# Raw weights and keys' copies issued by ScalarE, six output weight blocks split in the last pair, and shared buffers for parts of the softmax units, in a one-core attention layer

## The chip, the core and the metric

The kernel runs on one core of a Trainium2 chip. The core has five engines, each with its own queue of instructions that it works through strictly in order: TensorE (PE, matmuls and weight loads), VectorE (DVE), ScalarE (ACT), GpSimd (POOL) and SyncE (SP, which here only issues DMAs). [...] An instruction that has to wait holds up everything behind it in its queue. The metric is the device time of one execution in microseconds (us), as the median of several runs.

## The reference

One transformer-like layer on a sequence of 1024 rows with 1024 features, all float32. Two attention groups of eight heads each read the same normalised input: softmax attention with a forget gate, and stick-breaking attention. Their outputs pass a SiLU gate and one output projection, and a residual with a final layer norm ends it.

```python
u = layer_norm(x) * (1 + scale) + shift            # shift, scale, gate from silu(c) @ w_ada + b_ada
fq, fk, fv, fg, ff, sq, sk, sv, sg = split(u @ w_in)
# softmax group, per head:   s = q k^T / 8 + (f_q - f_k), causal;  p = softmax(s);  o = p v
# stick-breaking, per head:  z = q k^T / 8;  w = exp(log_sigmoid(z) + sum of later log_sigmoid(-z));  o = w v
y = concat(o_fox * silu(fg), o_sb * silu(sg)) @ w_out
out = layer_norm(2 ** 0.25 * x + gate * y) * ln_g + ln_b
```

## The kernel before, in words

Precision: most float32 products are made of rounded parts. A matrix is split into a high part (rounded) and a low part (the rest), and three matmuls (high by high, low by high, high by low) stand for one. `fetch_w` (L134) does this for weights: a DMA brings a raw block of 128x512 into one of two `wraw` buffers, POOL rounds it into `whi` (L141) and subtracts to get `wlo` (L142); the five-deep ring `whi`/`wlo` feeds PE. For output weights POOL first multiplies the raw block by the gate (L139).

Heads are worked in eight pairs; pairs 0 to 3 are stick-breaking, pairs 4 to 7 softmax. A pair has 16 units: one unit is one head and one block of 128 queries, `i` from 0 to 7, and its row of scores is (i+1)*128 wide. Pairs 0 to 3 go through the blocks upwards, pairs 4 to 6 downwards, widest first.

One softmax unit (`att_scores`, L492, and `halves`, L474) goes like this. PE makes the scores `S` (L504, L505) in one of two PSUM buffers. DVE reads them with the forget term `fb` into `a` and finds the row bound `nm` (L511). ACT takes the exponential (L517). ACT and DVE make two 16-bit halves of the result in a buffer `f` (L483, L484). SP issues a transposing DMA from `f` to `pt` (L488). Four units later PE multiplies `pt` by the values (`pv`, L582). Both `a` and `f` come from a ring of six buffers named `att`, which also holds `fb`; a buffer is free again when its last reader is done, for `f` the transposing DMA. A stick-breaking unit uses `kp` and `be` from the same ring, with a scan on DVE and a product on POOL (L538).

Between the matmuls of the units PE is given "filling" work: the projections of later pairs (`gen_m`, lines L288 to L290, `m`, which produce queries, keys and gates; `gen_v`, L359 to L361, `v`, values). A table FILL says how many steps of filling each pair gets, and a weight per unit says how they are spread over its 16 units. `v_finish` scales the values; it ends in a small matmul `vsum` (L397) that waits for DVE. `forget_rows` makes the cumulated forget gates (`fcum`, L431), for which POOL prepares a triangle of ones first. The order of PE's instructions is written out by hand; on DVE, ACT, POOL and SP the framework's scheduler orders them, by its own estimate of when each is ready.

Keys (`evac_k`) are copied by ACT out of PSUM, and a small DMA copies each half to the other 64 partitions (L270, issued by SP). Values and other big buffers share a ring `v` of three 8 KB buffers.

Output weights: from the end of pair 3 through pair 6 `gen_split_out` (L927) fetches all eight blocks of `w_out` in two halves each, splits them on POOL and stores both parts to a DRAM scratch `wo_dr` (L933, L934). In the last pair, PE's filling is the last gate projection (`gen_last_g`), step `kt` by step. Each step frees the buffers `u{kt}` and `v{kt}` (the normalised input), and `load_wo(kt)` brings block `kt` back from `wo_dr` into them (L924, L925). Then the output projection (`o_step`, L986 to L988) of row tile 6 begins, `gen_out_first`, block by block, and the other seven row tiles follow. `load_y` brings the stored gated outputs back and splits them on POOL, through the same `wraw` and `whi`/`wlo` buffers.

## Time and profile before

| | |
|---|---|
| median of 3 runs | 699.71 us (699.4 to 701.07) |
| the profiled execution | 706.99 us, of which the span from first to last instruction is 705.3 us |
| mean granted TensorE clock in it | 0.956 of full speed |
| DVE busy | 497.7 us (71%) |
| ACT busy | 397.1 us (56%) |
| POOL busy | 414.3 us (59%) |
| first scores of pairs 0, 4, 5, 6, 7 | at 89.6, 340.5, 423.2, 492.6 and 565.0 us |

How to read it: the profile page lists, for the whole span, the busy time of each engine, and the wait lists say which engine stood idle, in front of which instruction, and which instruction ended that idle time. "PE S L504 <- DVE nm L511" is PE standing in front of the score matmul of line 504 until DVE's line 511 was done. In tables by window, the columns are the window, its length, the busy time of PE, PE's weight loads, DVE, ACT and POOL (with instruction counts), the TensorE clock granted (1.00 is full), the DMA engines' busy share and their GB/s. An engine name with a q ("SPq", "ACTq") is that engine's queue issuing a DMA.

### The profile page before, as it was taken

Reading aid. Unit: us, or ns where it says so; the run is one execution under the profiler, and the core shown is the slowest. Engines: PE = TensorE matmul, PEld = TensorE weight load, DVE = VectorE, ACT = ScalarE, POOL = GpSimd, SP = SyncE. Lnnn points to the kernel's source line nnn. Section 1 sums busy time; section 2 is a strip of 40 time slices with the busy share of each in tenths; the row PEclk is TensorE's granted clock in tenths of the full one; section 3 lists DMA queues with packets and bytes.
Section 4 is the critical chain, followed back from the end, with each engine's and each line's share of the span. In section 5 each row is a group of like instructions: output and inputs, shape, how many; then the busy total and the mean of one; then the engine's idle time right before and its main releaser. Section 6 shows DMA issues by size and latency. Waiting matters only on the chain.

```text
span 705.3 us, 10983 instructions
## 1 busy us (share of the span) xinstructions
PE 639.4 (91%) x3531; PEld 532.7 (76%) x3531; DVE 497.7 (71%) x924; ACT 397.1 (56%) x788; POOL 414.3 (59%) x499
## 2 busy tenths in 40 slices
PE   6999998999988999979898699899879786999995
PEld 4788897888977778869786578699658574687885
DVE  6885368868688887986886736676748756677645
ACT  5568367858585767856755635555546655541000
POOL 6559966757389667663874577655753111376511
PEclk9999999999999999999998989899899898899998
DMA  9966321135536465553678765879784799996311
GB/s 335 409 248 204 93 70 43 42 53 129 102 79 146 96 144 122 136 129 75 183 192 198 189 181 157 222 184 237 174 215 105 154 313 280 255 194 192 98 60 60
DMA packets 177641, 114.58 MB, mean 162 GB/s; under 512 B 137840, under 2 KB 151472, under 8 KB 177584
## 3 DMA queue, kind: packets, MB, share of 16 engines
q1 hardware_dynamic: 176144, 109.68, 59.6%
q10 hardware_dynamic: 1440, 4.21, 1.9%
q8 instruction: 28, 0.46, 0.3%
q14 instruction: 29, 0.24, 0.1%
HBM read 60.34 MB, written 16.29 MB: 109 GB/s over the span
## 4 chain that ended last, share of the span: by engine, by line
PE 64%; DMA 13%; DVE 10%; POOL 4%; issue 4%; ACT 3%; SPq 2%; ACTq 0%; DVEq 0%; POOLq 0%
PE m L288 7%; PE m L290 7%; PE m L289 7%; PE pv L582 6%; DMA pt<-f 6%; PE o L988 4%; PE o L987 4%; PE o L986 4%; PE S L504 3%; PE S L505 3%; PE v L359 3%; PE v L361 3%; PE v L360 3%; DVE kp L481 2%; DMA raws<-in_w_qkg_dram 1%
## 5 line engine op out<-in xcount | busy, mean ns | idle before, releaser
L288 PE MATMUL m<-uh,whi 128*128 128x512 f32 x304 | 130.4, 429 | 12.3 <-POOL whi L141 11.0
L290 PE MATMUL m<-uh,wlo 128*128 128x512 f32 x304 | 124.9, 411 | 1.4 <-POOL wlo L142 1.4
L289 PE MATMUL m<-ul,whi 128*128 128x512 f32 x304 | 124.5, 410 | 0.0
L538 POOL TENSOR_TENSOR be<-be,kp 128x127 f32<-128x127 f32 (+3 forms) x64 | 85.9, 1343 | 33.8 <-DVE kp L534 18.4
L611 POOL TENSOR_TENSOR ty<-ty,sg 64x256 f32<-64x256 f32 x64 | 51.0, 797 | 89.1 <-DVE ty L609 67.7
L484 DVE SCALAR_TENSOR_TENSOR f<-a,l,f 128x1024 f16<-128x1024 f32 (+3 forms) x64 | 61.1, 955 | 32.7 <-ACT f L483 32.0
L504 PE MATMUL S<-k,q 128*128 128x512 f32 (+5 forms) x192 | 67.3, 352 | 12.5 <-DVE nm L511 12.5
L288 PEld LDWEIGHTS m<-uh,whi 128*128 128x128 f32 x304 | 60.4, 199 | 24.2 <-POOL whi L141 12.3
L517 ACT ACTIVATE a<-a,nm 128x1024 f32<-128x1024 f32 (+3 forms) x64 | 49.6, 776 | 48.0 <-DVE nm L511 47.4
L290 PEld LDWEIGHTS m<-uh,wlo 128*128 128x128 f32 x304 | 60.3, 198 | 17.7 <-POOL wlo L142 3.1
L530 DVE TENSOR_TENSOR_SCAN kp<-kp,floor 128x512 f32<-128x512 f32 (+2 forms) x64 | 65.1, 1017 | 12.0 <-ACT kp L524 10.8
L483 ACT ACTIVATE f<-a,l 128x1024 f16<-128x1024 f32 (+3 forms) x64 | 49.7, 776 | 40.8 <-DMA pt<-f 19.4
L582 PE MATMUL pv<-pt,v 128*128 128x256 f16 (+1 forms) x560 | 69.2, 274 | 0.0
L481 DVE TENSOR_TENSOR kp<-be,kp 128x128 f16<-128x128 f32 (+7 forms) x48 | 55.8, 1164 | 17.3 <-ACT kp L480 16.6
L289 PEld LDWEIGHTS m<-ul,whi 128*128 128x128 f32 x304 | 60.7, 200 | 9.6
L511 DVE CUSTOM_DVE_ANT_0 a<-S,fb 128x1024 f32<-128x1024 f32 (+3 forms) x64 | 48.2, 753 | 26.4 <-DMA pt<-f 20.1
L505 PE MATMUL S<-kl,qz 128*128 128x512 f32 (+5 forms) x192 | 66.5, 347 | 0.0
L582 PEld LDWEIGHTS <-v 128*128 128x128 f16 x560 | 50.4, 102 | 17.9 <-issue 10.3
L359 PE MATMUL v<-whi_v,uh 128*128 128x256 f32 (+1 forms) x192 | 56.1, 292 | 6.1 <-DVE kl L272 5.0
L361 PE MATMUL v<-wlo_v,uh 128*128 128x256 f32 (+1 forms) x192 | 55.0, 286 | 0.5 <-POOL wlo_v L142 0.5
L360 PE MATMUL v<-whi_v,ul 128*128 128x256 f32 (+1 forms) x192 | 54.8, 285 | 0.0
L142 POOL TENSOR_TENSOR wlo<-raw,whi 128x512 fp32r<-128x512 f32 x38 | 52.7, 1389 | 1.6
(316 smaller groups left out, 1579.2 us busy)
## 6 DMA issues: line engine op xcount, KB each, us to landing
raw<-in_w_qkg_dram SPq DMA_DIRECT2D x38, 256.0 KB, 2.9
wss<-in_w_ss_dram SPq DMA_DIRECT2D x16, 512.0 KB, 8.4
k<-k SPq DMA_DIRECT2D x32, 128.0 KB, 2.4
wg<-in_w_gate_dram SPq DMA_DIRECT2D x8, 512.0 KB, 5.0
raw_o<-in_w_out_dram SPq DMA_DIRECT2D x16, 256.0 KB, 3.4
fb<-f_dr ACTq DMA_DIRECT2D x8, 512.0 KB, 4.6
wo_dr<-whi_o SPq DMA_DIRECT2D x16, 256.0 KB, 2.3
wo_dr<-wlo_o SPq DMA_DIRECT2D x16, 256.0 KB, 2.5
```

Source lines behind the costliest of these rows:

```text
L288: nc.tensor.matmul(acc, hi[:, c], u_hi[kt][:, s], start=(kt == 0), stop=False)
L289: nc.tensor.matmul(acc, hi[:, c], u_lo[kt][:, s], start=False, stop=False)
L290: nc.tensor.matmul(acc, lo[:, c], u_hi[kt][:, s], start=False, stop=(kt == NB - 1))
L359: nc.tensor.matmul(acc[:, :n], u_hi[kt][:, ts_], hi[:, s], start=(kt == 0), stop=False)
L360: nc.tensor.matmul(acc[:, :n], u_lo[kt][:, ts_], hi[:, s], start=False, stop=False)
L361: nc.tensor.matmul(acc[:, :n], u_hi[kt][:, ts_], lo[:, s], start=False, stop=(kt == NB - 1))
L481: nc.vector.tensor_tensor(second, a3, first, op=ALU.subtract)
L504: nc.tensor.matmul(S[:, s, :w], qst[p][h][:, qs], kst[p][h][:, ks], start=True, stop=False)
L505: nc.tensor.matmul(S[:, s, :w], z, klo[p][:, ks], start=False, stop=True)
L530: scan = nc.vector.tensor_tensor_scan(rv, rv, floor[0][:, 512 - n:][:, ::-1], initial=0.0, op0=ALU.mult, op1=ALU.max)
L538: nc.gpsimd.tensor_tensor(be[:, :ke - 1], be[:, :ke - 1], kp[:, 1:ke], op=ALU.mult)
L582: nc.tensor.matmul(acc[:, q0:256], vt[p][:, kb, h * P:h * P + P], st_pt[p, h, j][:, 2 * kb + part, q0:], start=start, stop=stop)
```

## The change

- **Who issues.** Raw blocks that have neither a gate to be multiplied in nor a home of their own are issued by ACT instead of SP: all weights of `gen_m` and `gen_v` and two early value blocks. The keys' copies of pairs 2 to 7 move to ACT too. In all, 52 raw loads and 24 copies stand in ACT's queue now.
- **Output weights.** Only blocks 0 and 1 (PRE = 2) are split ahead, around the start of pair 4, and stored to DRAM. Blocks 2 to 7 are fetched, multiplied (POOL), rounded (now by ACT) and subtracted (POOL) in the last pair, straight into `u{pr-2}` and `v{pr-2}`. Blocks 0 and 1 come back from DRAM into a `v` buffer and two `q` buffers.
- **Buffers.** In pair 4, in the first half of pair 5 and in nearly all of pair 6, the halves `f` of two units share one 8 KB `v` buffer instead of taking two `att` buffers.
- **Filling by size.** From pair 4 on a unit's share of filling is (6 + width in blocks) instead of (100 + width), so wide units get more and narrow ones less.
- **Timing of small steps.** `vsum` comes two steps later (VSTEP 3); `fcum`'s matmuls come three steps after its POOL work, which begins two steps earlier (FROW 10); the first output row tile begins one unit later (OUT0 5) and takes both halves of a block together; the loads of the norm's gain and bias and of `y` move by some units.

```diff
-    FROW = 12
+    FROW = 10
-    VSTEP = 1
+    PRE = 2
+    VSTEP = 3
...
-    def fetch_w(key, src, n, scale=None, home=None):
+    def fetch_w(key, src, n, scale=None, home=None, cast=None):
         raw = raw_tile(f"raw_{key}")[:, :n]
-        nc.sync.dma_start(raw, src)
+        (nc.sync if home or scale is not None else nc.scalar).dma_start(raw, src)
         if scale is not None:
             nc.gpsimd.tensor_tensor(raw, raw, scale, op=ALU.mult)
         hi, lo = home or ring_w(key)
-        nc.gpsimd.tensor_scalar(hi[:, :n], raw, 1.0, 1.0, op0=ALU.mult, op1=ALU.mult)
+        if cast:
+            cast(hi[:, :n], raw)
+        else:
+            nc.gpsimd.tensor_scalar(hi[:, :n], raw, 1.0, 1.0, op0=ALU.mult, op1=ALU.mult)
...
-            nc.sync.dma_start(kf[o, s], kf[r, s])
+            (nc.scalar if p >= 2 else nc.sync).dma_start(kf[o, s], kf[r, s])
...
+        for _ in range(3):
+            yield
         fp = acc_tile("fcum")
...
-            halves(u, a, att_tile(f"f_{p}_{h}_{i}"), l)
+            if p == 4 or (p == 5 and h == 0) or (p == 6 and (h or i < 6)):
+                if i % 2:
+                    room_ff[0] = sb.tile([P, 2, D], F32, tag="v", bufs=3, name=f"f_{p}_{h}_{i // 2}")
+                room = room_ff[0][:, i % 2, :]
+            else:
+                room = att_tile(f"f_{p}_{h}_{i}")
+            halves(u, a, room, l)
...
     def load_wo(pr):
-        hi = big(f"u{pr}", 1, f"woh_{pr}", F32R)
-        lo = big(f"v{pr}", 1, f"wol_{pr}", F32R)
-        nc.sync.dma_start(hi.bitcast(F32), wo_dr[0, pr])
-        nc.sync.dma_start(lo.bitcast(F32), wo_dr[1, pr])
+        if pr < 2:
+            if pr == 0:
+                both = sb.tile([P, 2, D], F32R, tag="v", bufs=3, name="wo_0")
+                hi, lo = both[:, 0, :], both[:, 1, :]
+            else:
+                hi, lo = (big("q", 4, f"wo{x}_{pr}", F32R) for x in "hl")
+        else:
+            hi = big(f"u{pr - 2}", 1, f"woh_{pr}", F32R)
+            lo = big(f"v{pr - 2}", 1, f"wol_{pr}", F32R)
+        if pr < PRE:
+            nc.sync.dma_start(hi.bitcast(F32), wo_dr[0, pr])
+            nc.sync.dma_start(lo.bitcast(F32), wo_dr[1, pr])
+        else:
+            for h in range(2):
+                s = slice(h * 512, h * 512 + 512)
+                fetch_w(f"o{pr}_{h}", w_out[pr * P:(pr + 1) * P, s], 512, gate[:, s], (hi[:, s], lo[:, s]), nc.scalar.copy)
...
-        for pr in range(NPAIR):
+        for pr in range(PRE):
...
-        for h in range(2):
-            for pr in range(NPAIR - 1):
+        for pr in range(NPAIR - 1):
+            for h in range(2):
                 o_step(t, h, pr)
...
-            load_wo(kt)
+            if kt + 2 < NB:
+                load_wo(kt + 2)
...
-    OUT0 = 4
+    OUT0 = 5
...
-        size = [W0 + u[2] + 1 for u in order(p)]
+        size = [(W0 if p < 4 else 6) + u[2] + 1 for u in order(p)]
...
         if k == LAST:
+            for pr in range(2):
+                load_wo(pr)
+        if k == LAST - 1:
             load_y(6)
+        if k == LAST + 5:
             load_ln()
```

How it moves instructions is seen at three places. In the names the numbers are pair, head and query block (for raw weights: pair, matrix and half), and the last number is the buffer's own.

SP's queue in the first half of pair 4, before: transposes of pair 4's units (`f_4_0_...`), the store of gated outputs, stores of output weights, and the raw keys' weights of pair 5.

```order
L488 DMA_TRANSPOSE pt_4_0_1_4083<-f_4_0_3_4080 128x8x128
L933 DMA wo_dr_95<-whi_o1_1_4219 128x512
L934 DMA wo_dr_95<-wlo_o1_1_4220 128x512
L488 DMA_TRANSPOSE pt_4_0_1_4083<-f_4_0_2_4143 128x6x128
L137 DMA raw_5_1_0_4259<-in_w_qkg_dram 128x512
L137 DMA raw_5_1_1_4265<-in_w_qkg_dram 128x512
L488 DMA_TRANSPOSE pt_4_0_0_4178<-f_4_0_1_4175 128x4x128
```

The same place now:

```order
L495 DMA_TRANSPOSE pt_4_0_1_4099<-f_4_0_1_4096 128x8x128
L632 DMA y_dr_94<-ty_3_1_3_4125 64x256
L495 DMA_TRANSPOSE pt_4_0_1_4099<-f_4_0_1_4096 128x6x128
L495 DMA_TRANSPOSE pt_4_0_0_4182<-f_4_0_0_4179 128x4x128
L632 DMA y_dr_94<-ty_4_0_3_4217 64x256
```

Only transposes and stores of gated outputs are left in SP's queue here; the pairs of units share one `f`.

ACT's queue at that place, before: the units' exponentials (`a`) and halves (`f`), and the copies of pair 5's queries out of PSUM.

```order
L517 ACTIVATE a_4_0_3_4072,l_4_0_3_4074<-a_4_0_3_4072,nm_4_0_3_4073 128x512
L462 CAST qz01_84<-q_4_0_3084 64x128
L483 ACTIVATE f_4_0_3_4080<-a_4_0_3_4072,l_4_0_3_4074 128x4x128
L517 ACTIVATE a_4_0_2_4135,l_4_0_2_4137<-a_4_0_2_4135,nm_4_0_2_4136 128x384
L259 ACTIVATE q_5_0_4086<-m_5_0_0_4088 64x512
```

And now:

```order
L524 ACTIVATE a_4_0_3_4088,l_4_0_3_4090<-a_4_0_3_4088,nm_4_0_3_4089 128x512
L138 DMA raw_5_1_0_4255<-in_w_qkg_dram 128x512
L490 ACTIVATE f_4_0_2_4000<-a_4_0_5_3992,l_4_0_5_3994 128x6x128
L490 ACTIVATE f_4_0_2_4000<-a_4_0_4_4043,l_4_0_4_4045 128x5x128
L621 ACTIVATE ty_3_1_3_4125<-pv_3_1_3_4108,bss_sb_101 64x256
L490 ACTIVATE f_4_0_1_4096<-a_4_0_3_4088,l_4_0_3_4090 128x4x128
L468 CAST qz01_84<-q_4_0_3084 64x128
L138 DMA raw_5_1_1_4261<-in_w_qkg_dram 128x512
L524 ACTIVATE a_4_0_2_4139,l_4_0_2_4141<-a_4_0_2_4139,nm_4_0_2_4140 128x384
```

The raw loads stand between the steps of the softmax units now, and each waits in ACT's queue until POOL has freed a raw buffer.

POOL's queue in the last pair, before: gated outputs (`ty`) and the splits of stored outputs (`yr`).

```order
L611 TENSOR_TENSOR ty_6_1_1_6323<-ty_6_1_1_6323,sg_6_5542 64x256
L966 TENSOR_SCALAR whi_y_6_4_6250<-yr_6_4_6248 128x384
L967 TENSOR_TENSOR wlo_y_6_4_6251<-yr_6_4_6248,whi_y_6_4_6250 128x384
L611 TENSOR_TENSOR ty_6_1_0_6404<-ty_6_1_0_6404,sg_6_5542 64x256
L611 TENSOR_TENSOR ty_7_0_3_6476<-ty_7_0_3_6476,sg_7_6172 64x256
```

Now, shown where the last two output blocks are split (`raw_o6`, `raw_o7`; `wol` is the low part, `woh` the high part that ACT has rounded):

```order
L140 TENSOR_TENSOR raw_o6_1_6226<-raw_o6_1_6226,gate_91 128x512
L146 TENSOR_TENSOR wol_6_6220<-raw_o6_0_6221,woh_6_6219 128x512
L146 TENSOR_TENSOR wol_6_6220<-raw_o6_1_6226,woh_6_6219 128x512
L140 TENSOR_TENSOR raw_o7_0_6253<-raw_o7_0_6253,gate_91 128x512
L140 TENSOR_TENSOR raw_o7_1_6258<-raw_o7_1_6258,gate_91 128x512
L146 TENSOR_TENSOR wol_7_6252<-raw_o7_0_6253,woh_7_6251 128x512
L146 TENSOR_TENSOR wol_7_6252<-raw_o7_1_6258,woh_7_6251 128x512
```

Twelve multiplications and twelve subtractions stand in POOL's queue of the last pair, where there were none; PE needs block 7 to finish row tile 6.

More of the change, by code (lines that the diff above doesn't have):

```diff
@@ L125, in tile_hybrid_layer @@
     y_dr = dr.tile([NPAIR, P, SEQ], F32, tag="y_dr", name="y_dr")
-    wo_dr = dr.tile([2, NPAIR, P, D], F32, tag="wo_dr", name="wo_dr")
+    wo_dr = dr.tile([2, 2, P, D], F32, tag="wo_dr", name="wo_dr")
     f_dr = dr.tile([8, SEQ], F32, tag="f_dr", name="f_dr")
@@ L471, in tile_hybrid_layer @@
     s_turn = [0]
+    room_ff = [None]
     def halves(u, a, room, l=None):
```

## The prediction

> **What bounds the kernel now.** I read the page's head and PE's row first, then the stages by window, then PE's waits, and last the clock behind each long wait.
>
> ```profile
> span 705.3 us, 10983 instructions
> PE 639.4 (91%) x3531; PEld 532.7 (76%) x3531; DVE 497.7 (71%) x924; ACT 397.1 (56%) x788; POOL 414.3 (59%) x499
> ```
>
> PE is busy for 91% of the span, and the change keeps its matmuls as they are. So only two things can be won: time in which PE stands still, and time in which it runs at a reduced clock. The stages (stick-breaking pairs; pairs 4 to 6; the last pair up to where output block 7 is in use):
>
> ```profile
> core 0: us, PE busy (x) PEld busy (x) DVE busy (x) ACT busy (x) POOL busy (x), PEclk, DMA share, GB/s
> 91.00:340.00 249.00, 234.64 (x1460) 205.25 (x1459) 199.95 (x274) 174.07 (x353) 164.10 (x214) 0.99 0.44 101
> 340.00:565.00 225.00, 197.09 (x1042) 160.60 (x1041) 152.60 (x369) 129.33 (x263) 132.55 (x124) 0.91 0.74 183
> 565.00:614.00 49.00, 38.92 (x187) 28.73 (x186) 30.26 (x75) 27.81 (x54) 9.46 (x13) 0.90 1.12 285
> ```
>
> Pairs 4 to 6 lose 225.0 - 197.1 = 27.9 us standing and 225 * 0.09 = 20 us by the clock; the next 49 us lose 10.1 and 4.9. Pairs 0 to 3 lose 14.4 and 2.5. No other engine is near its limit there (DVE 68% in pairs 4 to 6). Who makes PE stand:
>
> ```profile
> PE S L504 <- DVE nm L511: 12.5, 4, 4.4
> PE m L288 <- POOL whi L141: 11.0, 3, 7.5
> PE v L359 <- DVE kl L272: 5.0, 1, 5.0
> PE vsum L397 <- DVE bss_sb L395: 4.3, 2, 2.4
> PE o L986 <- issue: 3.2, 1, 3.2
> PE o L986 <- DMA woh<-wo_dr: 2.8, 2, 1.7
> PE fcum L431 <- POOL be L539: 2.7, 1, 2.7
> PE o L988 <- DMA wol<-wo_dr: 2.4, 3, 1.5
> PE m L290 <- POOL wlo L142: 1.4, 3, 0.7
> PE vsum L397 <- DVE pt L563: 1.3, 1, 1.3
> ```
>
> And the clock in the 6 to 8 us that begin where such a wait ends (windows, PEclk third from the end):
>
> ```profile
> 205.30:212.00 6.70, 6.70 (x26) 5.29 (x27) 6.49 (x9) 6.59 (x10) 6.19 (x8) 0.75 0.44 108
> 311.85:318.00 6.15, 6.15 (x38) 6.15 (x38) 3.76 (x7) 3.82 (x10) 2.81 (x5) 0.72 1.00 204
> 345.36:352.00 6.64, 6.64 (x29) 5.57 (x29) 4.15 (x10) 6.58 (x8) 5.88 (x7) 0.74 0.58 147
> 379.87:388.00 8.13, 7.57 (x26) 5.28 (x27) 3.32 (x8) 3.88 (x7) 3.20 (x4) 0.58 0.83 147
> 407.02:415.00 7.98, 7.83 (x28) 5.68 (x29) 1.65 (x6) 1.74 (x5) 6.89 (x7) 0.74 0.58 151
> 446.65:454.00 7.35, 7.35 (x23) 5.83 (x24) 6.22 (x18) 6.50 (x15) 2.37 (x4) 0.63 0.85 214
> 495.09:503.00 7.91, 7.06 (x24) 4.87 (x25) 4.74 (x14) 4.93 (x7) 5.81 (x5) 0.59 0.60 174
> 523.47:530.00 6.53, 6.53 (x33) 5.07 (x33) 5.09 (x16) 3.41 (x8) 0.73 (x1) 0.74 0.86 195
> 559.03:567.00 7.97, 7.79 (x29) 5.80 (x29) 5.77 (x20) 4.07 (x12) 0.73 (x1) 0.64 0.80 175
> ```
>
> Each wait is paid for twice: length times (1 - clock) gives 1.7, 1.7, 1.7, 3.4, 2.1, 2.7, 3.2, 1.7 and 2.9 us.
>
> **Part 1: raw weights no longer queue behind SP's work.** The longest wait, 7.5 us, ends at 407.02. In time (start, duration, engine):
>
> ```profile
> 403.24 1.07 SPq L137 DMA_DIRECT2D raw<-in_w_qkg_dram  x2
> 406.34 0.62 POOL L141 TENSOR_SCALAR whi<-raw 128x512 fp32r<-128x512 f32 x1 [8.69 <-DMA raw<-in_w_qkg_dram]
> ```
>
> POOL stood idle 8.7 us for a block that landed 3.1 us after its issue: most of the wait lay ahead of the issue, in SP's queue. Now ACT issues it, between the softmax steps of units that came earlier, and POOL loses the split of six blocks in pairs 4 to 6, which stood ahead of the projections' splits and took the raw and ring buffers:
>
> ```profile
> L142 POOL TENSOR_TENSOR wlo_o<-raw_o,whi_o 128x512 fp32r<-128x512 f32 x16 | 24.7, 1544 | 2.2 <-DMA wo_dr<-wlo_o 1.6
> L139 POOL TENSOR_TENSOR raw_o<-raw_o,gate 128x512 f32<-128x512 f32 x16 | 23.6, 1480 | 14.2 <-DMA raw_o<-in_w_out_dram 14.2
> L141 POOL TENSOR_SCALAR whi_o<-raw_o 128x512 fp32r<-128x512 f32 x16 | 13.1, 818 | 5.9 <-DMA wo_dr<-whi_o 5.2
> ```
>
> That is 12 * (1.54 + 1.48 + 0.82) = 46 us of POOL's 133 busy us there. I take the waits on `whi` and `wlo` as gone: 11.0 + 1.4, and the clock behind 379.87, 407.02 and 495.09 (3.4 + 2.1 + 3.2): 21.1 us. The cover is one projection's length of prefetch; without it the wait is back in full.
>
> **Part 2: `f` in `v` buffers.** The `nm` waits come from the `att` ring. Before the one that ends at 446.65, ACT stood 7 us in front of a unit's `f`:
>
> ```profile
> 443.75 0.94 ACT L483 ACTIVATE f<-a,l 128x768 f16<-128x768 f32 x1 [6.99 <-DMA pt<-f]
> ```
>
> It waited for a transposing DMA to free a buffer, and DVE behind it could not take the next scores. With `f` elsewhere, `a` has the four buffers that `fb` leaves to itself. The three long waits (446.65 in pair 5's first half, 523.47 and 559.03 in pair 6) all lie where the change moves `f`. SP's transposes also lose the stores and raw loads that stood between them. I take 12.5 less the 0.7 us that falls in the last pair, so 11.8, and the clock 2.7 + 1.7 + 2.9: 19.1 us. Filling by size (about one more projection step behind the widest units, one less behind the narrow) keeps PE's work as it is; I cost it at nothing, covered by the two PSUM score buffers.
>
> **Part 3: small steps later.** Matmuls of 512 columns start 0.23 us apart at full clock:
>
> ```profile
> 612.10 0.40 PE L988 MATMUL o<-wol,whi_y 128*128 128x512 f32 x1
> 612.33 0.40 PE L986 MATMUL o<-woh,y7h 128*128 128x512 f32 x1
> ```
>
> `vsum` (4.3 + 1.3, clock 1.7 + 1.7) and `fcum` (2.7) get two and three more filling steps in front, each of six such matmuls, so 2.8 and 4.2 us against single waits of 2.4 and 2.7 us: 11.7 us gone. In return the values of pairs 4 and 5 are scaled later; `pv` of pair 4 comes six units in, which hides it.
>
> The TensorE clock, weighed: the rows show 0.75 and 0.74 behind waits of only 1.9 and 2.4 us (the two `vsum` waits, 4.3 us in all). [...]
>
> **Part 4: the last pair.** What goes are the waits on `wo_dr` and on issue (3.2 + 2.8 + 2.4) and their clock. What comes is a chain on POOL. PE frees the first home at 562.7 us, with the gate projection's step 0, and uses block 7 at 612.3 (`y7h`, above):
>
> ```profile
> 562.71 0.63 PE L288 MATMUL m<-uh,whi 128*128 128x512 f32 x1
> raw_o<-in_w_out_dram SPq DMA_DIRECT2D x16, 256.0 KB, 3.4
> L611 POOL TENSOR_TENSOR ty<-ty,sg 64x256 f32<-64x256 f32 x64 | 51.0, 797 | 89.1 <-DVE ty L609 67.7 <-issue 14.2 <-DVE l L519 3.7
> ```
>
> That is 49.6 us. With two raw buffers, a block's cycle from the end of one first subtraction to the next is load 3.4, two multiplications 2.96 and a subtraction 1.54: 7.9 us (ACT's rounding hides behind the second multiplication). Block 2 takes 1.5, five more cycles 39.5, the last half 1.5, and about eight other POOL steps of 0.8 us 6.4: 48.9 us. So I expect the last pair to gain nothing: PE waits for POOL instead of DMA. If the loads are wholly hidden, 48.9 - 5 * (3.4 - 1.54) = 39.6, a gain of 10; if SP issues each block's loads late by as much as a load takes, 5 * 3.4 = 17 us are lost.
>
> **Part 5: what ACT takes on.** 76 issues and 12 roundings. An issue on ACT is seen once per half pair:
>
> ```profile
> 533.76 0.33 ACTq L448 DMA_DIRECT2D fb<-f_dr  x1
> ```
>
> 76 * 0.33 = 25 us on an engine with 44% to spare; hidden. The waits are not so safe. SP's queue stood in front of raw loads for POOL to free a buffer:
>
> ```profile
> SPq L137 <- POOL wlo L142: 33.0, 17, 5.2
> SPq L137 <- POOL be L539: 18.6, 10, 4.8
> ```
>
> Those 51.6 us now stand in ACT's queue, where scores, exponentials and PSUM copies queue behind and PE waits for them. Ends: nothing, or all 51.6. I take a quarter, 13 us, since a wait of ACT reaches PE only when it outlasts the two score buffers, that is two units (225 us / 48 units, so 9.4 us), and the longest is 5.2. For stalls that appear elsewhere (a pair's start, where the first `f` takes the buffer that pair 4's values want) I add 3.
>
> At the start two value blocks (0.52 MB) are now loaded ahead of x. The first two slices of the page move 335 and 409 GB/s:
>
> ```profile
> GB/s 335 409 248 204 93 70 43 42 53 129 102 79 146 96 144 122 136 129 75 183 192 198 189 181 157 222 184 237 174 215 105 154 313 280 255 194 192 98 60 60
> ```
>
> Cost 0 to 1.6; I take 1.3.
>
> **Sum.** -21.1 - 19.1 - 11.7 + 0 + 13 + 3 + 1.3 = -34.6 us. On the profiled execution's own time, 706.99, that is 672.4; the median of the runs is 7.3 us lower, so 699.7 - 34.6 = 665. The 5.0 us wait on `kl` I leave in.
>
> **Rivals.**
> 1. *ACT becomes the queue that stalls (slower).* The 51.6 us reach PE in full, with the 25 us of issue behind them for want of slack: 699.7 - 51.9 + 51.6 + 25 + 4.3 = 729; the point of decision is 48 us of new PE waits (51.9 - 4.3), where the gain is gone; halfway between there and the end, 714. For it: ACT's exponential and PSUM copies gate PE. Against: no wait of PE on ACT is among the ten longest. Chance 0.12.
> 2. *The raw blocks land no earlier.* If the DMA engines and not SP's queue hold them back (busy share 0.83 behind the wait at 379.87), part 1 is worth nothing: 665 + 21 = 686. [...] Against it: 3.1 us to land, after 8.7 us idle. Chance 0.12.
> 3. *The last pair's POOL chain is late*, by the upper end above: 665 + 17 = 682. For it: SP puts raw loads behind transposes. Chance 0.16.
> 4. *Everything fits*: no cost on ACT (13 + 3), the `kl` wait gone with 1.7 us of clock, 10 us in the last pair: 665 - 33 = 632. Chance 0.10.
>
> The forecast itself (650 to 678) has 0.50.
>
> **From cases to numbers.** 0.3% of 699.7 is 2.1 us, about what a measurement of this kernel can tell from no change. Faster by more: the forecast, rivals 2 to 4, less 0.03 for combinations of 2 and 3 with part of 1: 0.85. Slower: 0.12, same 0.03. The range leaves out rival 1 and the far half of rival 4: 640 to 700.
>
> **What would show it.** Right: no `m <- POOL whi` wait over 2 us in pairs 4 to 6; no `S <- nm` wait in pair 5's first half or pair 6; clock of 340 to about 530 us at 0.97 or more; `vsum` and `fcum` gone from PE's list; PE waiting for POOL's `wol` at blocks 6 and 7. Wrong: ACT's raw issues waiting on POOL for over 30 us in sum with PE behind; the stage of pairs 4 to 6 still over 205 us long; block 7 in use more than 55 us after the first home is free.

## The result, and the profile after

| | before | after |
|---|---|---|
| median of 3 runs | 699.71 us (699.4 to 701.07) | 691.04 us (689.68 to 693.09) |
| the profiled execution, its span | 706.99, 705.3 us | 689.68, 688.0 us |
| granted TensorE clock in it | 0.956 | 0.968 |

The change made the kernel faster by 1.3%: ratio 0.987, 95% interval 0.983 to 0.992. The direction was forecast and the time lies in the range, but the gain is 8.7 us where 34.6 were forecast. Part of the difference lies in the times of before: in the five batches told below, the kernel before came to medians of 703.3 to 707.0 us (7 to 19 runs each, single runs from 697.7 to 715.6), so its first three runs were low and its profiled execution was not. From profile to profile the change is worth 17.3 us, half of the forecast. Medians in this document are over all runs, while ratios leave out runs in a slower state, such as one of a_no_gate's four, 769.88 us at a clock of 0.75, without which its median is 673.98 us.

The head of the page after, and its stages by window (to the first scores of pair 0, of pair 4, of pair 7, to block 7's first use, to the end):

```profile
span 688.0 us, 10896 instructions
PE 630.0 (92%) x3531; PEld 526.3 (76%) x3531; DVE 491.0 (71%) x924; ACT 402.2 (58%) x800; POOL 402.1 (58%) x487
```

```profile
core 0: us, PE busy (x) PEld busy (x) DVE busy (x) ACT busy (x) POOL busy (x), PEclk, DMA share, GB/s
0.00:91.90 91.90, 84.32 (x427) 68.12 (x428) 55.82 (x98) 51.40 (x84) 65.92 (x96) 1.00 0.69 249
91.90:337.80 245.90, 235.75 (x1474) 205.88 (x1473) 194.17 (x275) 175.69 (x355) 166.14 (x215) 0.99 0.47 103
337.80:531.80 194.00, 182.79 (x1038) 152.47 (x1037) 145.45 (x367) 128.38 (x265) 87.31 (x88) 0.98 0.69 161
531.80:592.60 60.80, 40.06 (x188) 29.28 (x186) 37.78 (x82) 35.37 (x69) 36.41 (x33) 0.83 0.87 189
592.60:688.00 95.40, 87.10 (x410) 70.51 (x410) 57.82 (x103) 11.40 (x28) 46.29 (x59) 0.95 0.36 115
```

Pairs 4 to 6 take 194.0 us where they took 224.6, at a clock of 0.98 instead of 0.91, and POOL works 87 us in them instead of 132. The next stage went the other way: 60.8 us for 47.3, with PE standing for a third of it and the clock at 0.83. PE's waits after, longest sum first:

```profile
PE o L1011 <- ACT woh L143: 9.6, 2, 6.4
PE S L511 <- DVE nm L518: 9.3, 5, 4.5
PE pv L595 <- DVE ty L622: 7.8, 5, 3.8
PE sc_all L185 <- POOL later L335: 4.9, 1, 4.9
PE o L1013 <- POOL wol L146: 3.6, 3, 2.1
PE m L292 <- DVE fc L442: 2.8, 1, 2.8
PE m L292 <- DVE kl L280: 2.2, 1, 2.2
PE v L363 <- DVE kl L276: 1.8, 1, 1.8
```

Every wait for `whi` and `vsum` is gone. Of the 9.3 us for `nm`, 8.3 now fall in the last pair, and the waits for `woh` and `wol` (rounded and rest part of a late output weight block) are new. So the time was taken out of the middle, and half of it was paid back at the end. To see which part did what, the parts were undone and done alone.

### The profile page after: what moved, and what is told of

It is laid out like the page before. It is cut to its first block, busy times and chain, and to the rows that moved or that the text cites. A ratio compares the mean times of both kernels' runs of the same rounds, so it can differ in the third digit from the quotient of the medians.

```text
span 688.0 us, 10896 instructions
## 1 busy us (share of the span) xinstructions
PE 630.0 (92%) x3531; PEld 526.3 (76%) x3531; DVE 491.0 (71%) x924; ACT 402.2 (58%) x800; POOL 402.1 (58%) x487
## 5 line engine op out<-in xcount | busy, mean ns | idle before, releaser
L292 PE MATMUL m<-uh,whi 128*128 128x512 f32 x304 | 126.1, 415 | 5.7 <-DVE fc L442 2.8
L293 PE MATMUL m<-ul,whi 128*128 128x512 f32 x304 | 121.4, 399 | 0.0
L294 PE MATMUL m<-uh,wlo 128*128 128x512 f32 x304 | 121.4, 399 | 0.0
L491 DVE SCALAR_TENSOR_TENSOR f<-a,l,f 128x1024 f16<-128x1024 f32 (+3 forms) x64 | 64.4, 1009 | 28.8 <-ACT f L490 28.0
L543 DVE TENSOR_TENSOR_SCAN kp<-kp,floor 128x512 f32<-128x512 f32 (+2 forms) x64 | 65.0, 1016 | 15.8 <-ACT kp L537 14.7
L595 PE MATMUL pv<-pt,v 128*128 128x256 f16 (+1 forms) x560 | 67.8, 270 | 8.3 <-DVE ty L622 7.8
L292 PEld LDWEIGHTS m<-uh,whi 128*128 128x128 f32 x304 | 58.3, 192 | 17.0 <-issue 5.7
L524 ACT ACTIVATE a<-a,nm 128x1024 f32<-128x1024 f32 (+3 forms) x64 | 49.5, 774 | 35.5 <-DVE nm L518 31.1
L294 PEld LDWEIGHTS m<-uh,wlo 128*128 128x128 f32 x304 | 58.3, 192 | 14.0
L293 PEld LDWEIGHTS m<-ul,whi 128*128 128x128 f32 x304 | 58.5, 192 | 9.3
L488 DVE TENSOR_TENSOR kp<-be,kp 128x128 f16<-128x128 f32 (+7 forms) x48 | 48.1, 1003 | 18.4 <-ACT kp L487 17.9
L537 ACT ACTIVATE kp<-S 128x128 f32<-128x128 f32 (+3 forms) x64 | 41.6, 651 | 21.4 <-PE S L512 14.9
```

The lines of the kernel that those rows point to most:

```text
L292: nc.tensor.matmul(acc, hi[:, c], u_hi[kt][:, s], start=(kt == 0), stop=False)
L293: nc.tensor.matmul(acc, hi[:, c], u_lo[kt][:, s], start=False, stop=False)
L294: nc.tensor.matmul(acc, lo[:, c], u_hi[kt][:, s], start=False, stop=(kt == NB - 1))
L491: nc.vector.scalar_tensor_tensor(second, a3, l, first, op0=ALU.mult, op1=ALU.subtract)
L543: scan = nc.vector.tensor_tensor_scan(rv, rv, floor[0][:, 512 - n:][:, ::-1], initial=0.0, op0=ALU.mult, op1=ALU.max)
L595: nc.tensor.matmul(acc[:, q0:256], vt[p][:, kb, h * P:h * P + P], st_pt[p, h, j][:, 2 * kb + part, q0:], start=start, stop=stop)
```

## The experiments

All at a glance: medians and their ratio to before on the same chip; then, from the profile of each, the stages as above ("last" is the last pair up to block 7's first use), and T0, the time from the end of the last gate projection's step 0, which frees the first home (the buffers that block 2 goes to; before the change, block 0), to that use.

| kernel | us | ratio (95%) | start | pairs 0-3 | pairs 4-6 | last | end | T0 |
|---|---|---|---|---|---|---|---|---|
| before, first profile | 699.7 | | 89.6 | 250.8 | 224.6 | 47.3 | 93.0 | 49.6 |
| b_again | 706.1 | 1.001 (0.996-1.006) | 90.0 | 248.9 | 219.5 | 46.5 | 93.4 | 49.1 |
| after, first profile | 691.0 | 0.987 (0.983-0.992) | 91.9 | 245.9 | 194.0 | 60.8 | 95.4 | 63.1 |
| a_again | 690.2 | 0.981 (0.974-0.988) | 92.8 | 246.2 | 190.6 | 63.5 | 95.8 | 64.9 |
| b_last_new | 692.3 | 0.986 (0.978-0.994) | 89.7 | 250.7 | 201.8 | 49.5 | 98.5 | 52.0 |
| b_f_v | 695.3 | 0.987 (0.979-0.994) | 89.6 | 247.7 | 208.3 | 52.4 | 96.1 | 53.8 |
| a_last_old | 701.4 | 0.997 (0.992-1.001) | 92.6 | 246.0 | 207.7 | 58.0 | 95.3 | 59.4 |
| a_f_att | 690.2 | 0.978 (0.970-0.987) | 91.5 | 246.2 | 200.8 | 52.0 | 99.5 | 54.4 |
| a_sp_issue | 683.9 | 0.974 (0.967-0.980) | 89.7 | 245.0 | 188.6 | 56.8 | 98.4 | 58.2 |
| a_steps | 685.8 | 0.972 (0.965-0.979) | 91.9 | 245.4 | 189.0 | 62.9 | 96.0 | 64.3 |
| a_fill100 | 686.9 | 0.976 (0.967-0.985) | 91.9 | 245.4 | 190.9 | 60.1 | 96.0 | 61.5 |
| a_two | 691.2 | 0.980 (0.974-0.986) | 89.6 | 247.7 | 191.6 | 57.6 | 99.1 | 59.0 |
| a_no_gate | 675.0 | 0.958 (0.951-0.966) | 92.0 | 247.6 | 189.0 | 48.6 | 95.1 | 50.0 |
| a_pre4 | 681.6 | 0.965 (0.958-0.972) | 92.0 | 245.9 | 194.0 | 52.4 | 96.9 | 53.8 |
| a_sp_pre4 | 681.9 | 0.968 (0.961-0.976) | 89.6 | 244.4 | 195.8 | 52.4 | 98.1 | 53.8 |
| a_pre8 | 699.5 | 0.992 (0.988-0.995) | | | | | | |
| a_raw_act | 688.7 | 0.976 (0.971-0.982) | 91.1 | 248.8 | 189.7 | 61.8 | 96.1 | 63.2 |
| a_cast_pool | 691.3 | 0.985 (0.980-0.990) | 92.2 | 247.5 | 191.1 | 63.1 | 94.8 | 65.4 |
| a_raw_pool | 692.7 | 0.985 (0.977-0.993) | 91.9 | 245.0 | 190.9 | 59.2 | 102.8 | 61.5 |
| a_raw_pool_y_act | 695.9 | 0.984 (0.977-0.992) | 91.7 | 246.3 | 192.9 | 62.8 | 103.5 | 65.3 |

### Both kernels again

**b_again**: before, unaltered.

> The kernel before, unchanged, profiled once more. Its first profiled execution took 706.99 us where the median of its runs is 699.7. Theory A (the gain of pairs 4 to 6 is real and is given back in the last pair): a second profile shows pairs 4 to 6 within 4 us of the first (224.6 us from the first scores of pair 4 to those of pair 7) and the 7 us lie elsewhere or in one wait. Rival B (part of the gain was only a bad draw): pairs 4 to 6 take 217 us or less, and 7 us of the waits I counted on are missing.

706.05 us, ratio 1.001. Its profiled execution took 700.2 us and has the same long waits (`nm` 11.3 us, `whi` 9.2). Pairs 4 to 6 take 219.5 us in it, 5.1 less than in the first, which lies between the two forecasts. The kernel before simply spreads, from 697.7 to 715.6 us.

**a_again**: after, unaltered.

> The changed kernel once more, unaltered, in the same batch as the three below and with the kernel before beside it on the same chip (which came to 705 to 707 us there in earlier batches, 699.7 in its first three runs). Theory A: the changed kernel repeats at 689 to 693, so its ratio to before is nearer 0.978 than the 0.987 first measured. Rival: it is spread like before and comes to 694 to 700, ratio 0.987 again.

690.24 us; the kernel after repeats, and beside seven runs of before (703.3) the ratio is 0.981.

### The output weights alone, and all but them

**b_last_new**: before, with the part on the output weights and the last pair's code only (PRE = 2, the new `load_wo` and its calls, `gen_out_first`, OUT0 = 5).

```diff
-        for pr in range(NPAIR):
+        for pr in range(PRE):
...
-            load_wo(kt)
+            if kt + 2 < NB:
+                load_wo(kt + 2)
```

> The kernel before with only the other half of the change: two output blocks split ahead, six in the last pair, new order of the output projection and late loads. Theory A: the last pair loses 12 to 18 us here too (from pair 7's first scores to PE's end 145 to 152 instead of 133), and pairs 4 to 6 win 10 to 15 us because POOL and SP no longer do the splits there: total about that of the kernel before, within 6 us. Rival (the last pair's loss needs the other parts): 133 to 138 us there and a total 8 us or more below before.

692.31 us. Pairs 4 to 6 lose 18 to 23 us against the two profiles of before, though raw weights are still issued by SP. The wait for `whi` in pairs 4 to 6, 11.0 and 9.2 us in before, is down to this row of its wait list:

```profile
PE m L292 <- POOL whi L145: 2.2, 1, 2.2
```

**a_last_old**: after, with that part undone (PRE = 8, `load_wo(kt)`, OUT0 = 4).

> The changed kernel, but everything about output weights and the last pair as before: eight blocks split ahead, brought back from DRAM step by step, old order of the output projection and of the late loads. Kept: raw weights and keys' copies on ACT, f in v buffers, filling by size, later small steps. Theory A (those parts won 25 to 30 us in pairs 4 to 6, and the new last pair gave 16 back): from the first scores of pair 7 to PE's end 131 to 136 us instead of 149, pairs 4 to 6 205 to 212 (some of the gain was POOL's relief), total 685 to 690. Rival (the last pair is slow because all before it got faster and it starts earlier): 145 us or more, total 697 or more.

701.35 us, ratio 0.997 with 1 inside the interval: without the output weights' move, nothing measurable is left of the change's gain in time. Pairs 4 to 6 are still 12 to 17 us shorter than in the two profiles of before (207.7 us), but the last pair is 11 longer and the start 3.

### The other parts undone

**a_sp_issue**

```diff
-        (nc.sync if home or scale is not None else nc.scalar).dma_start(raw, src)
+        nc.sync.dma_start(raw, src)
-            (nc.scalar if p >= 2 else nc.sync).dma_start(kf[o, s], kf[r, s])
+            nc.sync.dma_start(kf[o, s], kf[r, s])
```

> The changed kernel with raw weights and keys' copies issued by SP again. By my part 1, the waits of PE on whi and wlo come back in pairs 4 to 6: 8 to 21 us slower than the changed kernel, 698 to 712. Rival (the relief came from the splits that left POOL and SP, not from who issues): 689 to 694.

683.85 us. The `whi` waits do not come back, but for one:

```profile
PE m L292 <- POOL whi L145: 4.0, 1, 4.0
```

The start is 2 us shorter, as in every kernel here in which SP issues the raw weights (89.6 to 90.0 against 91.1 to 92.8). Issuing from ACT had a price in pairs 4 to 6 too. In after, ACT's and then PE's timeline:

```profile
381.55 0.19 ACT L524 ACTIVATION_READ_ACCUMULATOR a<-a,nm 128x1 f32 x1
386.88 0.34 ACTq L138 DMA_DIRECT2D raw<-in_w_qkg_dram  x1
387.39 1.15 ACT L490 ACTIVATE f<-a,l 128x1024 f16<-128x1024 f32 x1 [5.66 <-POOL wlo L146]
388.56 0.47 ACT L621 ACTIVATE ty<-pv,bss_sb 64x256 f32<-64x256 f32 x1
```

```profile
390.30 0.93 PE L595 MATMUL pv<-pt,v 128*128 128x256 f16 x8 [3.83 <-DVE ty L622]
```

ACT stands at the issue of a raw load, from 381.7 to 386.9 us, until POOL's `wlo` has freed the raw buffer; `ty`, which frees the accumulator that PE wants for `pv`, is queued behind it, and PE stands 3.8 us.

**a_f_att**

```diff
-            if p == 4 or (p == 5 and h == 0) or (p == 6 and (h or i < 6)):
+            if False:
```

> The changed kernel with part 2 undone: f is taken from the att buffers again in every unit; all else as changed. Theory A (my part 2): the f buffers are what made PE wait for nm in pairs 4 to 6, so these waits come back there (8 to 12 us, before had 11.8) and pairs 4 to 6 take 205 to 213 us where the changed kernel takes 194. Since PE then reaches the last pair later, the last pair gets some of it back (block 7 in use 50 to 58 us after the first home is free, changed: 63.1); time 697 to 710. Rival B: the waits for nm hang on ACT's queue and not on buffers, so part 2 is worth nothing: pairs 4 to 6 within 3 us of 194, time 689 to 693. Rival C: f in v buffers holds up the values of the next pair; then without it pairs 4 to 6 are shorter than 191 and the time is under 688.

690.18 us, as much as after. The `nm` waits of pairs 4 to 6 come back (6.8 us, after: 1.1) and these pairs take 200.8 us, but the last pair takes 52.0. Its two windows:

```profile
337.70:538.60 200.90, 187.84 (x1039) 155.11 (x1038) 148.91 (x363) 127.94 (x262) 89.62 (x88) 0.96 0.72 168
538.60:590.50 51.90, 37.09 (x187) 27.59 (x186) 38.55 (x87) 36.17 (x72) 38.09 (x33) 0.89 0.72 167
```

So part 2 does what it says and loses it again behind. None of the three times forecast for this run came; what part 2 does to the last pair is taken up below.

**b_f_v**: before, with part 2 alone (the same condition put in).

> The kernel before with part 2 of the change alone: f of pair 4, of pair 5's first half and of most of pair 6 in the values' buffers. Theory A (my part 2): the waits for nm in pairs 4 to 6 (11.8 and 11.3 us in two profiles) go to under 3 us, pairs 4 to 6 fall from 222 to 203 to 208 us, and the last pair, whose end hangs on the reloads from DRAM, gives some of it back: time 688 to 697. Rival B: POOL's splitting of the output weights and SP's queue hold the raw weights and keep PE waiting in any case, the nm waits go but waits for whi grow by as much: 702 to 708. Rival C: the full 19 us: 684 to 688.

695.32 us, a gain of 8 us (ratio 0.987): no `nm` wait is left in pairs 4 to 6, which lose 11 to 16 us, and the last pair takes 5 to 6 more.

**a_steps**: VSTEP = 1, FROW = 12, no three steps ahead of `fcum`.

> The changed kernel with part 3 undone: VSTEP 1, FROW 12, no three steps ahead of fcum. Theory A (my part 3): the waits for vsum (5 us in two) and fcum (2.7) come back with a few us of slow clock; time 696 to 703. Rival B: only the waits come back and the last pair absorbs half of them, since it waits for DVE and POOL anyway: pairs 4 to 6 longer by 3 to 6 us, time 691 to 695. Rival C: the waits hung on when POOL and DVE were free, which the rest of the change altered: no vsum wait over 1 us, time 689 to 692.

685.76 us. The waits come back (`vsum` 4.6 and 1.3, `fcum` 1.7 us), and the slow clock behind them comes back too. The longest `vsum` wait and the 6.6 us behind it, and then the same stretch of after, which has no such wait:

```profile
342.18 0.58 PE L401 MATMUL vsum<-bss_sb,ones 128*128 128x1 f32 x2 [2.42 <-DVE bss_sb L399]
342.18:348.82 6.64, 6.64 (x21) 5.01 (x22) 3.66 (x9) 5.08 (x6) 6.48 (x8) 0.51 0.61 177
```

```profile
342.18:348.82 6.64, 6.42 (x32) 5.08 (x31) 3.59 (x11) 5.78 (x8) 5.64 (x7) 1.00 0.63 162
```

Yet no stage before the last pair is longer for it, because other waits are missing: PE's waits on `ty` in front of `pv` in pairs 4 to 6 are 0.8 us where after has 7.2, and the 2.8 us wait on `fc` of after's list is not there. Why part 3 brings the waits on `ty` is not shown.

**a_fill100**: `size = [W0 + u[2] + 1 ...]` for all pairs.

> The changed kernel with only the filling by size undone: W0 (100) for all pairs, so each unit of pairs 4 to 6 gets about the same filling again. Theory A (filling by size is why units lag less in pairs 4 to 6): large units then have too little filling behind them, PE waits for nm again, pairs 4 to 6 take 198 to 206 us (194 in the changed kernel), time 693 to 700. Rival B (it is a cost): large units come last in a half pair, so filling by size leaves their transposes and pv later, which hands the last pair a longer queue; without it the last pair's stretch from first scores to block 7 falls from 60.8 to under 56, time 683 to 688. Rival C: no difference, 689 to 693 with all stages within 2 us.

686.85 us, all stages within about 3 us of after. Filling by size does nothing that can be seen here.

**a_two**: `a_sp_issue`, `a_steps` and `a_fill100` in one, so that only the output weights and part 2 are left of the change.

> The changed kernel reduced to two of its parts: the output weights (two blocks ahead, six in the last pair) and f in the values' buffers. Raw weights and keys' copies are issued by SP, VSTEP 1, FROW 12, no steps ahead of fcum and even filling, all as before. Theory A: the other parts are worth nothing or cost (undone one by one they gave 683.9, 686.9, 685.8 against 690 to 691): 679 to 686, pairs 4 to 6 at 188 to 196. Theory B (the prediction's): raw weights on ACT and later steps each carry part of the gain in pairs 4 to 6, and one by one the others cover for them; without all of them whi and vsum waits come back together: pairs 4 to 6 over 200, time 692 to 700.

691.24 us, ratio 0.980, as after (0.981). Pairs 4 to 6 take 191.6 us, so these two parts carry the whole gain there. This kernel differs from b_last_new in part 2 alone: pairs 4 to 6 are 10.2 us shorter for it, the last pair is 8.1 longer. That the three came out 4 to 7 us faster one by one and not together says how far single batches of four runs can be trusted: their intervals overlap that of after.

### Why the last pair is long

**a_no_gate**: POOL's multiplication by the gate left out for the six late blocks.

```diff
-        if scale is not None:
+        if scale is not None and not cast:
```

> The changed kernel without POOL's multiplication of the six late output weight blocks by the gate (12 steps of 1.3 us left out; the output then lacks the gate on these blocks). Theory A: lateness of the loads on SP sets the chain, POOL's own work is slack: stage within 3 us of 60.8, time 687 to 692. Rival B (the prediction's chain of 48.9 us of POOL work): the chain shortens by 5 to 6 cycles of 2 * 1.3, 13 to 16 us: block 7 47 to 51 us after the first home, time 675 to 680.

675.04 us: T0 falls from 63.1 to 50.0, and of the waits for `woh` and `wol` (13.2 us) 1.4 us are left. So in after the blocks' chain through POOL, and not the softmax units, ends this stage.

**a_pre4**: PRE = 4, two more blocks split ahead, and **a_pre8**: PRE = 8, all of them.

> The changed kernel with four output blocks split ahead instead of two, so four instead of six in the last pair. Theory A (in the last pair each block costs a cycle of 8 to 12 us and block 7 is late by them): block 7 is in use about two cycles, 16 to 24 us, earlier than 62.7 us after the first home is free, or as early as PE itself gets there (about 45), the time falls to 672 to 680, less some 3 us that come back in pairs 4 and 5 from POOL's and SP's extra work. Rival (the splits ahead were what the waits of pairs 4 to 6 were made of): pairs 4 to 6 grow by 10 us or more and the time stays at 688 to 694.

> The changed kernel with all eight output blocks split ahead and brought back from DRAM, as in the kernel before; all other parts of the change stay. Theory A: the last pair takes about what it took before (block 7 some 48 to 53 us after the first home is free instead of 62.7), pairs 4 to 6 give back a third of their 30 us, total 682 to 688. If the splits ahead were the whole cause of the waits in pairs 4 to 6: these are back near 220 us and the total is 697 to 703.

681.61 and 699.53 us. With four blocks left for the last pair it is shorter (52.4), and the two more splits cost nothing that can be seen in pairs 4 to 6 (194.0). With a_sp_pre4, below, this is the fastest kernel here with the full computation; its interval (0.958 to 0.972) lies below that of after (0.974 to 0.988). With all eight split ahead and brought back, the gain is nearly gone (its profiled execution took 706.7 us, 7 more than its median, so its stages are not compared).

**a_sp_pre4**: `a_sp_issue` and `a_pre4` together.

> The changed kernel with two edits: raw weights and keys' copies issued by SP as before the change, and four output weight blocks (not two) split ahead and fetched back. Alone they gave 683.9 and 681.6 (changed: 691.0). Theory A: they act on different places (ACT's queue in pairs 4 to 6 and at the start; POOL's chain in the last pair), so the gains add: 671 to 676, start 89.7, pairs 4 to 6 at 189, the last pair's stretch to block 7 at 50 to 53. Rival B: both gains come out of the same last-pair slack, or SP's queue, which has all issues and four reloads again, delays the reloads behind transposes (PE waits on wo_dr over 8 us): 680 to 685. Rival C: with SP issuing all again, two more splits bring the waits for whi back (over 5 us in pairs 4 to 6): 686 or more.

681.87 us: the two do not add. In the last pair PE stands 7.1 us for block 0's reload here, and 8.2 us in a_pre4.

**a_raw_act**: the late blocks' raw loads issued by ACT. **a_cast_pool**: their rounding on POOL instead of ACT.

> The changed kernel with the raw output blocks of the last pair issued by ACT instead of SP, so that they do not stand behind transposing DMAs. If SP's order is what makes the cycle long (the transposes ahead of a load wait for their own units): block 7 comes about 8 us earlier, total 681 to 686. If POOL's own work and the two raw buffers set the cycle: no change, 689 to 693. If ACT's queue then stands in front of the loads and holds up the units: slower, 693 to 700.

> The changed kernel with the last pair's six output blocks rounded by POOL instead of ACT. If ACT's queue is held up there (a rounding waits for POOL's multiplication and the units' exponentials queue behind it): the waits of PE on DVE's nm in the last pair shrink to under 4 us, but POOL's chain grows by 12 times 0.7 = 8 us; total 684 to 692. If ACT's roundings hold up nothing: block 7 comes 6 to 8 us later and the total is 696 to 699.

688.72 and 691.32 us; the last pair takes 61.8 and 63.1. In the first, ACT stood 3.8 us with a rounding that waited for POOL, and an exponential behind it started 5 us after its bound was ready.

**a_raw_pool**: those raw loads issued by POOL. **a_raw_pool_y_act**: besides, y's slices loaded by ACT.

```diff
-        (nc.sync if home or scale is not None else nc.scalar).dma_start(raw, src)
+        (nc.gpsimd if cast else nc.sync if home or scale is not None else nc.scalar).dma_start(raw, src)
-            nc.sync.dma_start(raw.rearrange("p (a q) -> p a q", q=P),     # second kernel only
+            nc.scalar.dma_start(raw.rearrange("p (a q) -> p a q", q=P),
```

> The changed kernel, with the raw loads of the last pair's six output weight blocks issued by POOL (which itself frees their buffers) instead of SP. Theory A: those loads are late because SP issues them behind transposes of f that stand for PE and DVE (raw loads at 554.6, 576.3 and 587.2 us, POOL then idle 2.9, 3.1 and 5.4 us): POOL's idle before raw_o falls from 28 us to under 18, block 7 is in use 50 to 56 us after the first home is free (changed: 63.1), time 679 to 686. Rival B: POOL's queue has its own steps to do ahead (be, ty, y's rounding) and the issue costs POOL time, so the gain is under 3 us: 688 to 692. Rival C: the softmax chain sets the end of the last pair, not the weight blocks: woh and wol waits go, nm and ty waits take their place, stage within 2 us of 60.8, 688 to 692.

> The changed kernel with the last pair's raw output weights issued by POOL (alone: 692.7) and the loads of y's slices by ACT, so that no load of the block chain stands behind SP's transposes. In the changed kernel y's first slice waits there: POOL stands 4.8 us for it at 551.8 with block 4 queued behind. Theory A: the chain is held by loads behind transposes: POOL's wait for y's first slice falls under 1.5 us, block 7 is in use 50 to 56 us after the first home is free (63 to 65 in two profiles, 61.5 with raw loads on POOL alone), time 678 to 686. Rival B: POOL's own order and the two raw buffers, which y's slices share, set the chain, and the loads' queue hardly matters: 59 us or more, time 688 to 694. Rival C: ACT stands for y's buffers and the exponentials behind it wait: nm waits over 12 us, 692 to 700.

692.71 and 695.91 us; T0 61.5 and 65.3. My reading that the last pair is long because SP issues these loads behind transposes falls. Counted from the moment the first home is free, block 4's second raw half is issued after 28.4 us in after, and after 26.6, 26.5 and 24.8 in a_raw_act, a_raw_pool and a_raw_pool_y_act; it has landed after 32.4 us in after, and after 34.4, 32.6 and 35.3 in these three. Issued somewhat earlier on another queue, it lands no earlier. POOL's timeline in the second kernel, and the window:

```profile
552.62 1.13 POOL L138 DMA_DIRECT2D raw_o<-in_w_out_dram  x2
562.95 1.26 POOL L140 TENSOR_TENSOR raw_o<-raw_o,gate 128x512 f32<-128x512 f32 x1 [9.21 <-DMA raw_o<-in_w_out_dram]
```

```profile
552.60:563.00 10.40, 4.79 (x30) 3.78 (x28) 3.49 (x8) 3.46 (x6) 1.19 (x4) 0.98 1.13 125
```

Issued at 552.6, the block lets POOL go on at 562.95, with the DMA engines' share at 1.13. What the load waited for in these 10 us is not shown.

### What part 2 does to the last pair

T0 is 52.0 and 54.4 in the two kernels that have the new output weight code without part 2 (b_last_new, a_f_att), and 58 to 65 in all with both, but for the three in which POOL has less to do there. One candidate for the reason is block 0. It comes back from DRAM into a buffer of the ring `v`. With part 2 that buffer holds `f` until the last units of pair 6. The list for the tile `wo` (block 0), after and then a_f_att:

```profile
L945 SPq DMA_DIRECT2D wo<-wo_dr x1: 537/537/537, 539.6 to 539.6; - x1
DMA to landing us min/median/max: 7.3/7.7/8.1
```

```profile
L945 SPq DMA_DIRECT2D wo<-wo_dr x1: 339/339/339, 491.4 to 491.4; - x1
DMA to landing us min/median/max: 3.5/4.2/5.0
```

In after, the 1 MB is issued 7.7 us into the last pair; in a_f_att it was issued 47 us before that pair began. What follows in after, on SP's queue and on POOL (in brackets: how long the engine stood before the row, and what ended it):

```profile
539.56 0.54 SPq L945 DMA_DIRECT2D wo<-wo_dr  x1
540.15 0.45 SPq L946 DMA_DIRECT2D wo<-wo_dr  x1
540.70 7.37 SPq L495 DMA_TRANSPOSE pt<-f  x1
548.17 0.54 SPq L988 DMA_DIRECT2D yr<-y_dr  x1
...
551.36 0.53 SPq L988 DMA_DIRECT2D yr<-y_dr  x1
...
554.58 0.52 SPq L138 DMA_DIRECT2D raw_o<-in_w_out_dram  x1
```

```profile
542.70 2.56 POOL L146 TENSOR_TENSOR wol<-raw_o,woh 128x512 fp32r<-128x512 f32 x2
...
551.77 0.62 POOL L991 TENSOR_SCALAR whi_y<-yr 128x512 fp32r<-128x512 f32 x1 [4.83 <-DMA yr<-y_dr]
...
557.93 1.26 POOL L140 TENSOR_TENSOR raw_o<-raw_o,gate 128x512 f32<-128x512 f32 x1
...
563.30 1.26 POOL L146 TENSOR_TENSOR wol<-raw_o,woh 128x512 fp32r<-128x512 f32 x1
...
590.62 1.26 POOL L140 TENSOR_TENSOR raw_o<-raw_o,gate 128x512 f32<-128x512 f32 x1 [5.37 <-DMA raw_o<-in_w_out_dram]
```

The transpose behind the 1 MB holds SP for 7.4 us, so y's first slice is issued at 548.2 and block 4's raw load at 554.6. y's slices use the same two raw buffers and stand ahead of block 4 on POOL, so block 3's subtraction begins at 542.7 and block 4's only at 563.3: 20.6 us for a cycle that I had put at 7.9. Not all of this is the late reload: with block 0 there in time, the same cycle takes 14.9 us in a_f_att (549.1 to 564.0) and 15.4 in b_last_new, so y's slices lengthen it in any case, and the reload can account for some 5 us.

That part 2 lengthens T0 is shown by kernels that differ in nothing else: 54.4 in a_f_att against 63.1 and 64.9 in after, 52.0 in b_last_new against 59.0 in a_two, so 7 to 10.5 us. That it does so through block 0's late reload is shown only in part. For it speaks a_pre4, where block 0 is what PE itself waits for:

```profile
556.94 0.77 PE L1011 MATMUL o<-wo,whi_y 128*128 128x512 f32 x1 [8.17 <-DMA wo<-wo_dr]
```

Against it as the whole reason: from before to b_f_v T0 grows by 4 to 5 us too (49.6 and 49.1 to 53.8), and there no output block uses the ring `v`. The path through SP's transpose and y's slices is read from the rows above and was not tried by itself: no run gave block 0 another buffer or took y out of the raw buffers. In a_raw_pool_y_act y's first slice was issued as early after the first home as in a_f_att (14.7 and 14.3 us), and T0 was 65.3; in a_raw_act the transpose behind the 1 MB held SP for 4.9 us, and T0 was 63.2.

One pattern of the table bears on this and is not explained. In the twelve kernels with six late blocks and the gate, pairs 4 to 6 and the last pair together take 245.4 to 255.7 us, eleven of them at least 249.2, while pairs 4 to 6 alone range from 188.6 to 201.8. So what is won in pairs 4 to 6 mostly comes back in the last pair.

## Why the prediction was right and wrong

**The sum, stage by stage**, profile to profile: start +2.3, pairs 0 to 3 -4.9, pairs 4 to 6 -30.6, last pair +13.5, rest +2.4, in all -17.3. The forecast had +1.3 for the start, -51.9 + 13 + 3 = -35.9 for what comes before the last pair (measured -35.5), and 0 for the last pair (measured +15.9 with the rest). So the size of the gain was right up to 531.8 us, but partly by luck: with the second profiles of both kernels the same stages give -28.5 to -38.6, and the terms were wrong one by one, as told below. The term that failed in size is part 4's: "So I expect the last pair to gain nothing." It lost 13.5 us, and 13.5 to 17.0 over two profiles of each kernel. The other 8.6 us are the baseline: I took a difference worked out on an execution of 706.99 us from the median of three runs 7.3 us below it, and after's profile lies 1.4 us below its own median.

**Part 1 (-21.1): the waits went, the cause falls.** The clause "Now ACT issues it" did nothing for them: with SP issuing again, pairs 4 to 6 take 188.6 us. What freed POOL and SP's queue was the subordinate clause, "POOL loses the split of six blocks in pairs 4 to 6"; alone, it takes 18 to 23 us out of these pairs. Rival 2 (the raw blocks land no earlier, so part 1 is worth nothing) was right that the new issuer brought nothing, and wrong on the waits. The absence of `whi` waits, which I had named as the sign, could not tell these two causes apart.

**Part 2 (-19.1): right where I looked.** `nm` waits 11.8 to 1.1 us in pairs 4 to 6. Alone it is worth 8 us of time, and on top of the rest nothing (a_f_att 690.18 us, a_again 690.24), since the last pair gives it back; that its buffers are those that block 0 needs may be part of the reason. I had seen that `f` would compete for these buffers, and put 3 us on it for the wrong place, pair 4's values.

**Part 3 (-11.7): right on the wait, wrong on its worth.** The `vsum` waits are gone in after, and a_steps shows that each was paid for twice, as forecast: the clock is 0.51 and 0.75 over the 6.6 and 6.7 us behind waits of 2.42 and 1.87 us, and 1.00 in the same stretches of after. `fcum` was not gone: 1.4 of its 2.7 us are left, and 2.8 us on `fc` came with it. What failed is that these savings add to the time: with part 3 undone, pairs 0 to 3 take 245.4 us (after 245.9) and pairs 4 to 6 189.0 (after 194.0 and 190.6).

**Part 4 (0, ends -10 and +17): the mis-sized term.** The chain of 48.9 us came out at 52.0 and 54.4 without part 2 and at 63.1 in after. From block 2's first subtraction (531.16) to block 7's (593.76) the five cycles take 62.6 us, not 39.5 with 6.4 for other POOL steps; in a_f_att they take 52.0 (537.88 to 589.86). I counted y's slices as POOL steps and forgot that they occupy both raw buffers for a cycle, and I had the reload of block 0 nowhere. So the last pair is ended by the blocks' chain through POOL, as forecast (without the gate's steps T0 falls to 50.0), but the chain is longer than its sum, and part 2 adds 7 to 10.5 us to it. How much of this is the reload of block 0 stays open. Rival 3 (+17, chance 0.16) is what happened in size; the mechanism that it named, SP putting raw loads behind transposes, does not set the end by itself: with these loads out of SP's queue T0 is 61.5 to 65.3.

**Part 5 (+13): right in kind.** ACT's waits for POOL's weight steps sum to 13.1 us in after (`wlo` 5.7 + 0.9 + 0.7, `wlo_o` 2.3 + 1.9, `wlo_v` 0.8 + 0.8) and there are none of these in a_sp_issue; PE stood 3.8 us behind the longest. With SP issuing, pairs 4 to 6 are 2 to 5 us shorter (188.6 against 190.6 and 194.0). Rival 1 is real and small: its 51.6 us became 13.1, with the splits out of the pairs in which ACT issues. The 2.3 us of the start were put at 1.3.

**What would show it**: `whi`, `vsum`, the clock of 0.97 or more came as right, and `nm` but for 0.2 us in pair 6; so did waits on `wol`, though the longest is on `woh`. `fcum` did not go from PE's list. Of the three signs of wrong, one came: block 7 in use 63 us after the first home is free (limit 55).

## What to carry to other kernels

Work that is moved has two prices, and each is read at its own place: here the gain lay where the six splits left, not in the new queue, and half of it was paid back where they landed. For a chain in a late, thinly covered stage, list every user of its buffers, reloads and other slices too, and ask of each buffer lent out earlier who wants it next. And subtract a difference that was worked out on a profile from that profile's time, with enough runs of the kernel before to know where it lies.

## What was not expected of the hardware

DVE's last step of a unit (`f`, L491) took up to four times as long where POOL worked beside it. In after, with a POOL subtraction running from 582.75 to 585.25, and in a_no_gate with POOL idle for most of it:

```profile
582.59 3.21 DVE L491 SCALAR_TENSOR_TENSOR f<-a,l,f 128x512 f16<-128x512 f32 x1
```

```profile
575.08 0.76 DVE L491 SCALAR_TENSOR_TENSOR f<-a,l,f 128x512 f16<-128x512 f32 x1
```

The same shape takes 3.21 and 0.76 us. The first is the largest of the eight steps of this shape in after; of the others there, two that POOL worked beside for nearly their whole length took 0.92 and 1.62 us, and two with POOL idle (at 435.33 and 497.41) 0.74 and 0.75. So the size varies among the steps beside POOL too, and what sets it is not shown. And block 4's two raw halves, issued by POOL in a_raw_pool_y_act, took 10.2 and 10.4 us to land (between 552 and 564 us), and 5.9 and 6.1 in a_raw_pool, where the same loads issued by SP in after took 3.3 and 4.0.
